# Copies of the bias rows with the 128 rows as outermost dimension, in a two-layer attention and feed-forward network

## The chip, the cores and the metric

The kernel runs on one core of one Trainium2 chip. The metric is the time of one execution on the device in microseconds (us), the median of the runs shown. A core has TensorE (PE; PEld is its weight load), VectorE (DVE), ScalarE (ACT), GpSimd (POOL) and SyncE (SP), and 16 DMA engines that move data. Most transfers here are issued by SP, one after the other, from one queue.

## What is computed

Two layers, each a mixer of attentions and a feed-forward net with a convolution, over 1024 tokens of width 1024, all in float32. What matters here is the first mixer and its biases: every attention adds a bias that depends on the distance of query and key alone.

```
def even_mixer(x, ...):                       # layer 0
    qa, ka, va, hb = split_cols(x @ w_in, ...)
    o_a = diff_attention(qa, ka, va, lam, bias_table[:, :4])
    o_b = dilated_mixture(hb, bias_table)     # 3 dilations (1, 4, 16) x 4 heads
    return concat(o_a, o_b) @ w_out

def banded_attention(q, k, v, max_dist, bias_tbl, dist_scale):
    dist = arange(blk)[:, None] + n_prev * blk - kj[None, :]
    bias = bias_tbl[t5_bucket(dist * dist_scale)]
    s = q @ k.T * D ** -0.5 + bias            # masked, softmax, times v
```

Layer 1 uses the same kind of bias with other heads (kinds "nat" and "win" below).

## The kernel before

A matrix product runs as three float32r products (high by high, high by low, low by high: `mm3`, lines 310, 312 and 314). A weight slab is loaded from DRAM by SP into one of two raw buffers (`wr`), ACT copies out its high part (`wh`, line 124) and DVE the low part (`wl`, line 125). ACT and DVE take their work in order, so a split that waits for its slab holds up all that stands behind it.

The even mixer goes through ten groups of heads: six dilated ones (three dilations, two pairs of heads each), then four of the difference attention. `dense` projects a group's v, q and k (48 matmuls of 512 columns each, tile `dn`) while `attend` does the scores (`sc`, line 757), the softmax and the products of the group before. The first group's projections run beside the making of the biases.

The biases go three steps. `bias_rows` (line 676) writes a table `R` in DRAM (in the trace `bias_rows`), one row per head, with the bias at every distance, kind after kind: it goes over the 5120 columns in ten pieces of 512, each with a load of a one-hot table (`th`, line 694, by POOL), a matmul (`sc`, line 696), a copy by ACT (`tl`, line 698) and a write by POOL (line 699). `skew` (line 702) copies a head's row 128 times into a DRAM tensor `sk_...`, so that `bias_tile` (line 712) can read it back with each partition shifted by one element. `skew` is called for "d0", "d1" and "d2" (the three dilations, four heads at a time, 384 columns), for "nat" (one head at a time, 1152 columns, eight heads) and for "win" (two heads at a time, 768 columns, four calls). The last four of "nat" and all of "win" are only read in layer 1.

All those copies are DRAM to DRAM and are issued by SP (`dma`, line 212), between the loads of weights. The order in which instructions stand on each engine is not the order of the code: the framework builds a schedule with a model of its own of what each instruction takes, and moves the copies to wherever the tables that they read are ready. `_row_kinds` (line 2014) gives the order of the kinds in `R`, and with it which of the ten pieces a copy waits for.

Of the kernel before, what the change touches and what calls it, by code (L numbers as in the profile page):

```python
# [192 lines left out]
class Net:  # L193
# [508 lines left out]
    def skew(self, kind, heads):  # L702

        off, w = ROWS[kind]
        t = self.dpool.tile([len(heads), 128, w], F32, name=f"sk_{kind}{heads[0]}")
        src = self.R[heads[0]:heads[0] + 1, off:off + w]
        self.dma(out=t, in_=bass.AP(tensor=src.tensor, offset=src.offset,
                                                  ap=[[ROWS_W, len(heads)], [0, 128], [1, w]]))
        for e, h in enumerate(heads):
            self.skews[kind, h] = t[e, :, :]  # L710

# [1301 lines left out]

def _row_kinds():
    kinds = {}
    n = np.arange(1152)
    kinds["nat"] = (1023 - n, (1023 - n) >= 0)
    n = np.arange(768)
    kinds["win"] = (639 - n, ((639 - n) >= 0) & ((639 - n) <= 511))
    n = np.arange(384)  # L2020
    dist = 255 - n
    ok = (dist >= 0) & (dist <= 128)
    kinds["d0"] = (dist, ok)
    kinds["d1"] = (dist * 4, ok)

    kinds["d2"] = (dist * 8, ok & (dist % 2 == 0))
    n = np.arange(2048)
    kinds["cmp"] = (n - 1039, (n - 1039) >= 0)
    return kinds


_KINDS = _row_kinds()
ROWS, ROWS_W = {}, 0
for _k, (_d, _v) in _KINDS.items():
# [80 lines left out]
```

## Time and profile before

| what | us |
|---|---|
| median of 3 runs | 2882.4 (2880.62 to 2885.14) |
| the profiled execution, whole | 2881.72 |
| its span | 2879.9 |
| PE busy in the span | 2691.6 (93%) |
| DVE / ACT / POOL busy | 1902.4 / 1341.0 / 528.4 |

The page is read as follows. The chain that ended last tells which engine the time hangs on, in shares of the span. Where that is one engine almost throughout, the stretches in which this engine is idle are looked for with the list of waits; the waits' releasers are followed to the engine, the line and in the end the transfer that came last; and the table by stretches tells what the DMA engines did meanwhile, as a mean busy share of all 16 (0.50 is half of them, or all half the time) and in GB/s, and at which clock PE was granted to run (1.00 is 2.4 GHz, 0.50 is 1.2 GHz).

### The profile page before, as it was taken

How to read it: one execution, taken by the hardware profiler on the slowest of the kernel's cores; microseconds unless marked ns; L12 is line 12 of the kernel's file. 1: busy time of each engine (PE TensorE's matmuls, PEld its weight loads, DVE VectorE, ACT ScalarE, POOL GpSimd, SP SyncE). 2: the span in 40 equal slices, each digit the busy share in tenths (PEclk: the TensorE clock that was granted, in tenths of full speed). 3: DMA queues.
4: the chain of work that ended last, by engine and by line, in shares of the span. 5: the costliest groups of instructions: out<-in, count | busy, mean ns of one | idle time of the engine just before them, and what ended most of it. 6: DMA issues, size and time to landing. Idle time of an engine off the chain costs nothing.

```text
span 2879.9 us, 37915 instructions
## 1 busy us (share of the span) xinstructions
PE 2691.6 (93%) x13415; PEld 2249.5 (78%) x13415; DVE 1902.4 (66%) x4139; ACT 1341.0 (47%) x2666; POOL 528.4 (18%) x673
## 2 busy tenths in 40 slices
PE   7299999979899999999999999899997999999998
PEld 5188888867788888888778788878786888888886
DVE  3155678878866666635563788778778766667346
ACT  3155566634444444312452588767644444444123
POOL 1011100022211111000101255444313111110002
PEclk8599999989899999999999999999998999999999
DMA  6211121412222224521432221021331222227121
GB/s 202 87 52 56 54 59 42 141 64 97 74 87 82 81 81 153 179 85 52 133 93 95 88 67 55 16 50 45 140 103 66 88 81 81 81 95 241 67 88 59
DMA packets 233612, 256.22 MB, mean 89 GB/s; under 512 B 49269, under 2 KB 189029, under 8 KB 233423
## 3 DMA queue, kind: packets, MB, share of 16 engines
q1 hardware_dynamic: 229199, 242.57, 26.0%
q0 software_dynamic: 4224, 11.23, 1.4%
q8 instruction: 106, 1.74, 0.3%
q14 instruction: 83, 0.68, 0.1%
HBM read 198.38 MB, written 65.60 MB: 92 GB/s over the span
## 4 chain that ended last, share of the span: by engine, by line
PE 80%; DVE 8%; SPq 3%; ACT 3%; issue 3%; DMA 2%; POOL 1%; DVEq 0%; POOLq 0%; ACTq 0%
PE u L310 9%; PE u L312 9%; PE u L314 9%; PE dn L310 6%; PE dn L312 6%; PE dn L314 6%; PE mm L312 6%; PE mm L310 6%; PE mm L314 6%; PE pt L980 4%; SPq L212 3%; PE sc L757 2%; PE po L1649 2%; PE sc L1593 1%; DVE g L288 1%
## 5 line engine op out<-in xcount | busy, mean ns | idle before, releaser
L446 ACT ACTIVATE wh<-wr 128x512 fp32r<-128x512 f32 x284 | 173.7, 628 | 564.6 <-PE u L312 298.0
L447 DVE TENSOR_TENSOR wl<-wr,wh 128x512 fp32r<-128x512 f32 x284 | 209.7, 752 | 99.4 <-ACT wh L446 98.5
L982 DVE TENSOR_TENSOR tl<-pt,th 128x512 fp32r<-128x512 f32 (+3 forms) x344 | 196.9, 587 | 32.7 <-ACT th L981 29.3
L981 ACT ACTIVATE th<-pt 128x512 fp32r<-128x512 f32 (+3 forms) x344 | 170.9, 517 | 98.2 <-PE pt L980 44.4
L370 DVE TENSOR_TENSOR x<-mm,x 128x1024 f32<-128x1024 f32 x64 | 78.3, 1223 | 173.9 <-PE mm L314 173.9
L627 POOL TENSOR_TENSOR x<-x 128x512 f32<-128x512 f32 x44 | 72.5, 1649 | 652.5 <-DVE x L626 652.5
L125 DVE TENSOR_TENSOR wl<-wr,wh 128x512 fp32r<-128x512 f32 (+3 forms) x118 | 94.5, 803 | 111.0 <-ACT wh L124 106.1
L298 POOL TENSOR_TENSOR x<-x,ln_b 128x1024 f32<-128x1024 f32 x25 | 60.1, 2403 | 546.3 <-ACT x L297 546.3
L446 ACT ACTIVATE wh<-s 128x512 fp32r<-128x512 f32 x132 | 83.5, 632 | 131.6 <-PE u L312 128.3
L124 ACT ACTIVATE wh<-wr 128x512 fp32r<-128x512 f32 (+3 forms) x118 | 77.2, 657 | 140.1 <-PE dn L312 65.6
L636 DVE SCALAR_TENSOR_TENSOR x<-x,cv,x 128x1023 f32<-128x1023 f32 x88 | 112.7, 1280 | 32.2 <-ACT x L633 32.2
L310 PE MATMUL dn<-xq0h,wh 128*128 128x512 f32 x176 | 73.6, 418 | 58.0 <-ACT kh L735 50.7
L761 DVE CUSTOM_DVE_ANT_0 s<-sc,bt 128x128 f32<-128x128 f32 (+3 forms) x192 | 81.6, 450 | 51.2 <-PE sc L757 29.7
L980 PE MATMUL pt<-ident,s 128*128 128x128 f32 x644 | 105.4, 278 | 0.9
L1013 POOL TENSOR_SCALAR s<-s,d_rd 128x128 f32<-128x128 f32 (+1 forms) x96 | 44.9, 485 | 280.6 <-DVE d_rd L1010 232.7
L447 DVE TENSOR_TENSOR wl<-s,wh 128x512 fp32r<-128x512 f32 x132 | 92.8, 703 | 0.1
L980 PEld LDWEIGHTS pt<-ident,s 128*128 128x128 f32 x644 | 76.3, 142 | 12.9 <-issue 5.5
L310 PEld LDWEIGHTS dn<-xq0h,wh 128*128 128x128 f32 x176 | 35.0, 199 | 65.0 <-ACT kh L735 51.0
L1593 PE MATMUL sc<-kh,q 128*128 128x256 f32 (+4 forms) x208 | 73.6, 359 | 11.0 <-DVE n_mx L761 8.3
L1649 PE MATMUL po<-tl,V 128*128 128x256 f32 x264 | 82.6, 333 | 0.0
L1649 PE MATMUL po<-th,V 128*128 128x256 f32 x264 | 76.2, 299 | 4.8 <-ACT th L981 4.8
L288 DVE SCALAR_TENSOR_TENSOR g<-x,ln_w,ln_g 128x1024 f32<-128x1024 f32 x32 | 76.9, 2404 | 5.7 <-ACT x L297 3.4
(541 smaller groups left out, 8817.1 us busy)
## 6 DMA issues: line engine op xcount, KB each, us to landing
wr<-in_ffn_w_up_dram SPq DMA_DIRECT2D x88, 512.0 KB
hid<-x SPq DMA_DIRECT2D x44, 512.0 KB
wr<-hid SPq DMA_DIRECT2D x44, 512.0 KB
wr<-in_ffn_w_down_dram SPq DMA_DIRECT2D x44, 512.0 KB
wr<-in_ev_w_in_dram SPq DMA_DIRECT2D x44, 256.0 KB
xres<-x SPq DMA_DIRECT2D x16, 512.0 KB
x<-xres SPq DMA_DIRECT2D x16, 512.0 KB
wr<-in_od_w_in_dram SPq DMA_DIRECT2D x15, 512.0 KB
```

The lines of the kernel that those rows point to most:

```text
L288: nc.vector.scalar_tensor_tensor(y, x, m, g, op0=OP.add, op1=OP.mult)
L310: nc.tensor.matmul(o, lhsT=sh, rhs=m[0], start=start, stop=False, **kw)
L312: nc.tensor.matmul(o, lhsT=sh, rhs=m[1], start=False, stop=False, **kw)
L314: nc.tensor.matmul(o, lhsT=sl, rhs=m[0], start=False, stop=stop, **kw)
L446: nc.scalar.activation(hi, v, AF.Copy)
L447: nc.vector.tensor_sub(lo, v, f32(hi))
L636: nc.vector.scalar_tensor_tensor(g[:, s:], c[:, :S - s], cv[:, 2 - s, f:f + 1], g[:, s:], op0=OP.mult, op1=OP.add)
L980: nc.tensor.transpose(pt[:k, e * 128:(e + 1) * 128], b, self.ident)
L981: nc.scalar.activation(th[:k, :n], pt[:k, :n], AF.Copy)
L982: nc.vector.tensor_sub(tl[:k, :n], pt[:k, :n], f32(th[:k, :n]))
L1593: nc.tensor.matmul(ps[:, :c1 - c0], lhsT=q, rhs=k[part][:, c0:c1], start=part == 0, stop=part == 1)
L1649: nc.tensor.matmul(po[:, :256], lhsT=v, rhs=parts[part][:, e * 256:(e + 1) * 256], start=first and e + part == 0, stop=last and e + part = ...
```

## The change

Two edits. In `skew`, source and destination are walked with the 128 copies as the outermost dimension and the heads inside it; before, the heads were outermost. The same bytes go to the same places, in as many pieces. In `_row_kinds`, the three dilated kinds get the first columns of `R` (0 to 1151), then "nat" (1152 to 2303), "win" (2304 to 3071) and "cmp" as before.

```
@@ skew
-        self.dma(out=t, in_=bass.AP(tensor=src.tensor, offset=src.offset,
-                                                  ap=[[ROWS_W, len(heads)], [0, 128], [1, w]]))
+
+        self.dma(out=t.rearrange("h r w -> r h w"), in_=bass.AP(tensor=src.tensor, offset=src.offset,
+                                                                ap=[[0, 128], [ROWS_W, len(heads)], [1, w]]))
@@ _row_kinds
     kinds = {}
-    n = np.arange(1152)
-    kinds["nat"] = (1023 - n, (1023 - n) >= 0)
-    n = np.arange(768)
-    kinds["win"] = (639 - n, ((639 - n) >= 0) & ((639 - n) <= 511))
     n = np.arange(384)
...
     kinds["d2"] = (dist * 8, ok & (dist % 2 == 0))
+    n = np.arange(1152)
+    kinds["nat"] = (1023 - n, (1023 - n) >= 0)
+    n = np.arange(768)
+    kinds["win"] = (639 - n, ((639 - n) >= 0) & ((639 - n) <= 511))
```

Since a copy waits for other pieces of `R` now, the schedule of the first stage comes out in another order. The first place is SP's queue in the first stage. Numbers behind a name tell buffers apart; `sk_d04` is the copy of dilation 0 from head 4, `wr_528` and `wr_534` are the second half of the v weights and the first half of the q weights of the second group. Before:

```order
L212 DMA sk_nat7_8020<-bias_rows_304 128x1x1152
L212 DMA sk_win0_8310<-bias_rows_304 256x1x768
L212 DMA sk_win2_8600<-bias_rows_304 256x1x768
L212 DMA sk_win4_8890<-bias_rows_304 256x1x768
L212 DMA sk_d04_470<-bias_rows_304 512x1x384
L212 DMA sk_win6_9180<-bias_rows_304 256x1x768
L212 DMA wr_528<-in_ev_w_in_dram 128x4x128
L212 DMA wr_534<-in_ev_w_in_dram 128x4x128
L212 DMA sk_d18_602<-bias_rows_304 512x1x384
L212 DMA sk_d212_1077<-bias_rows_304 512x1x384
L212 DMA bt_517<-sk_d04_470 128x256 x2
L212 DMA bt_941<-sk_d04_470 128x256 x2
```

After, from the end of the first group's weights on:

```order
L212 DMA sk_d04_470<-bias_rows_304 128x4x384
L212 DMA sk_d18_602<-bias_rows_304 128x4x384
L212 DMA sk_d212_1077<-bias_rows_304 128x4x384
L212 DMA wr_455<-in_ev_w_in_dram 128x4x128
L212 DMA bt_517<-sk_d04_470 128x256 x2
L212 DMA bt_941<-sk_d04_470 128x256 x2
L212 DMA sk_nat0_1558<-bias_rows_304 128x1152
L212 DMA sk_nat1_2017<-bias_rows_304 128x1152
L212 DMA sk_nat2_2446<-bias_rows_304 128x1152
L212 DMA sk_nat3_2912<-bias_rows_304 128x1152
L212 DMA sk_nat4_7150<-bias_rows_304 128x1152
L212 DMA wr_528<-in_ev_w_in_dram 128x4x128
```

and behind that:

```order
L212 DMA sk_nat5_7440<-bias_rows_304 128x1152
L212 DMA sk_nat6_7730<-bias_rows_304 128x1152
L212 DMA sk_nat7_8020<-bias_rows_304 128x1152
L212 DMA sk_win0_8310<-bias_rows_304 128x2x768
L212 DMA wr_534<-in_ev_w_in_dram 128x4x128
L212 DMA sk_win2_8600<-bias_rows_304 128x2x768
L212 DMA sk_win4_8890<-bias_rows_304 128x2x768
L212 DMA sk_win6_9180<-bias_rows_304 128x2x768
L212 DMA wr_619<-in_ev_w_in_dram 128x4x128
L212 DMA wr_625<-in_ev_w_in_dram 128x4x128
```

The dilated copies and the bias tiles of the first two groups of heads 4 to 7 (`bt`) have moved from behind all others to the front; `wr_528` stands behind five copies of "nat", `wr_534` behind the eighth and one of "win", and `wr_619` and `wr_625` behind all.

The second place is PE in the first stage, where `sc_376` is the matmul of the seventh piece of `R` (its one-hot table is `th_374`) and `pt_...` are the transposes of the last input tiles. Before:

```order
L696 MATMUL sc_369<-th_367,tblp_306 16x512
L240 MATMUL pt_232<-ident_67,s_230 128x128 x4
L696 MATMUL sc_376<-th_374,tblp_306 16x512
L240 MATMUL pt_239<-ident_67,s_230 128x128 x4
L240 MATMUL pt_248<-ident_67,s_246 128x128 x4
L696 MATMUL sc_390<-th_388,tblp_306 16x512
L240 MATMUL pt_255<-ident_67,s_246 128x128 x4
L310 MATMUL dn_381<-xq2h_126,wh_275 128x512
```

After, further on in the q projection of the first group:

```order
L314 MATMUL dn_457<-xq1h_124,wl_292 128x512
L310 MATMUL dn_457<-xq1h_124,wh_291 128x512
L312 MATMUL dn_457<-xq1l_125,wh_291 128x512
L314 MATMUL dn_457<-xq1h_124,wl_292 128x512
L696 MATMUL sc_376<-th_374,tblp_306 16x512
L310 MATMUL dn_457<-xq1h_124,wh_291 128x512
L312 MATMUL dn_457<-xq1l_125,wh_291 128x512
L312 MATMUL dn_381<-xq2l_127,wh_275 128x512
L314 MATMUL dn_381<-xq2h_126,wl_276 128x512
```

All sixteen of those transposes and nineteen matmuls of the projections stand ahead of `sc_376` now; before, four of the transposes did.

## Rows read from the trace of the kernel before

**Rows 1.** The page's fourth part: the chain that ended last, by engine.
```profile
PE 80%; DVE 8%; SPq 3%; ACT 3%; issue 3%; DMA 2%; POOL 1%; DVEq 0%; POOLq 0%; ACTq 0%
```

**Rows 2.** Waits of PE, 20 to 150 us (total us, times, longest).
```profile
PE dn L310 <- ACT kh L735: 50.7, 1, 50.7
PE sc L696 <- DMA th<-in_c_onehot_dram: 9.3, 1, 9.3
PE sc L757 <- DVE dm L761: 7.7, 2, 7.4
```

**Rows 3.** PE, in time (start, us, instruction, idle before and releaser).
```profile
35.97 0.59 PE L696 MATMUL sc<-th,tblp 97*16 97x512 f32 x1 [9.32 <-DMA th<-in_c_onehot_dram]
...
120.35 0.80 PE L310 MATMUL dn<-xq0h,wh 128*128 128x512 f32 x1 [50.75 <-ACT kh L735]
...
121.37 0.63 PE L314 MATMUL dn<-xq0h,wl 128*128 128x512 f32 x1
121.79 0.63 PE L310 MATMUL dn<-xq0h,wh 128*128 128x512 f32 x1
...
126.81 0.39 PE L310 MATMUL dn<-xq1h,wh 128*128 128x512 f32 x1
127.03 0.39 PE L312 MATMUL dn<-xq1l,wh 128*128 128x512 f32 x1
```

**Rows 4.** ACT, in time, 60 to 124 us.
```profile
118.28 1.40 ACT L124 ACTIVATE wh<-wr 128x512 fp32r<-128x512 f32 x2 [52.47 <-DMA wr<-in_ev_w_in_dram]
```

**Rows 5.** SP's queue, in time, 18 to 140 us: start and time of issue.
```profile
23.33 1.87 SPq L212 DMA_DIRECT2D sk_nat<-bias_rows  x3
...
27.86 3.73 SPq L212 DMA_DIRECT2D sk_nat<-bias_rows  x5
37.70 31.11 SPq L212 DMA_DIRECT2D sk_win<-bias_rows  x3
68.91 14.84 SPq L212 DMA_DIRECT2D sk_d<-bias_rows  x1
83.80 11.40 SPq L212 DMA_DIRECT2D sk_win<-bias_rows  x1
95.30 14.86 SPq L212 DMA_DIRECT2D wr<-in_ev_w_in_dram  x2
...
119.04 10.04 SPq L212 DMA_DIRECT2D bt<-sk_d  x4
```

**Rows 6.** Stretches: length, busy us (instructions) by engine; then PEclk, DMA share, GB/s.
```profile
28.00:30.00 2.00, 0.00 (x0) 0.00 (x0) 0.70 (x2) 0.58 (x2) 0.42 (x1) 0.90 0.80 221
...
34.00:36.00 2.00, 0.03 (x1) 0.06 (x2) 0.00 (x0) 0.00 (x0) 0.00 (x0) 0.50 1.11 339
...
38.00:40.00 2.00, 1.87 (x8) 1.16 (x6) 1.38 (x2) 0.67 (x3) 0.00 (x0) 0.54 0.72 177
...
72.00:76.00 4.00, 0.00 (x0) 0.00 (x0) 0.00 (x0) 0.00 (x0) 0.00 (x0) 0.75 0.13 52
...
88.00:92.00 4.00, 0.00 (x0) 0.00 (x0) 0.00 (x0) 0.00 (x0) 0.00 (x0) 0.50 0.26 103
```

**Rows 7.** The same view, later stretches.
```profile
136.20:142.46 6.26, 5.92 (x18) 4.81 (x19) 5.50 (x23) 4.48 (x13) 1.76 (x4) 0.52 0.17 49
...
250.00:350.00 100.00, 100.00 (x544) 85.95 (x543) 59.46 (x154) 58.26 (x149) 16.04 (x36) 1.00 0.20 57
```

**Rows 8.** POOL, in time, 14 to 56 us: loads of the one-hot table.
```profile
25.34 1.77 POOL L694 DMA_DIRECT2D th<-in_c_onehot_dram  x3 [5.73 <-PE sc L696]
```

**Rows 9.** The chain that ended last, in time (start, us, what).
```profile
27.10 10.59 DMA bias_rows<-tl
```

**Rows 10.** DMA issues by line, with their count and size.
```profile
sk_nat<-bias_rows SPq DMA_DIRECT2D x8, 576.0 KB
sk_win<-bias_rows SPq DMA_DIRECT2D x4, 768.0 KB
wr<-in_ev_w_in_dram SPq DMA_DIRECT2D x44, 256.0 KB
```

## The prediction

> **What bounds the kernel now.** I read the chain that ended last first: PE holds 80% of it, SP's queue 3% [rows 1]. So time is won where PE stands idle, and the list of PE's waits says where in the first 150 us: 50.7 us for ACT's `kh`, 9.3 us for a one-hot table, 7.7 us for DVE's maxima `dm` [rows 2]. Later nothing of the kind comes: from 250 to 350 us PE is busy for 100.00 of 100 us [rows 7]. What PE gains early it should therefore keep.
>
> Then I follow the largest wait back. PE stops at 69.6 us and goes on at 120.35 [rows 3]. ACT has not written `kh` because a weight split stands ahead of it in its order, and that split waited 52.47 us for its slab `wr` [rows 4]. The slab was late on SP's queue: eight copies of "nat" (one head each) were issued in about 0.6 us apiece, but three of "win" (two heads each) held the queue for 31.11 us, one of `sk_d` 14.84, the last of "win" 11.40, and only then, at 95.30, came the two slabs [rows 5]. The table by stretches says why. While "nat" was moving, the DMA share was 0.80 to 1.11 and 221 to 339 GB/s; with only "win" under way it was 0.13, or 2 of 16 engines, and 52 GB/s; when the dilated copy had joined, 0.26, 4 of 16, and 103 GB/s [rows 6]. A copy is spread by its outermost dimension: two heads use two engines, four use four, 128 rows use all. The queue is held because these few engines are backed up. The 7.4 us behind the first wait are of one cause with it: the bias tiles were issued at 119.04 behind the dilated copies [rows 5], and DVE could not make its maxima without them.
>
> **The change part by part.** The new outer dimension is 128 for every copy, so I take "win" and the dilated copies to move as "nat" did. Terms, against the profiled execution (2881.7 us whole; the median of the runs is 2882.4, 0.7 above):
>
> 1. The 50.75 us wait goes if the slabs land before PE asks (checked below).
> 2. The 7.7 us wait for `dm` goes: the dilated copies and their bias tiles are now first in the queue, needing only the first three pieces of `R`, which were what "nat" needed before, issued at 23.33 [rows 5], so the bias tiles are there before 40 us, and PE wants them near 60.
> 3. After each long idle PE ran at half clock: 512-column matmuls start 0.42 to 0.43 us apart after 121 us, and 0.22 to 0.23 us apart at full clock [rows 3]. Eleven starts of the first stretch lose 0.2 us each, 2.3 us; the stretch from 136.20 to 142.46 (granted clock 0.52, 18 matmuls) [rows 7] loses about 2.4. Together 4.7 us, which go with the idles.
> 4. The 9.3 us wait was for the seventh one-hot table, issued with two others at 25.34 [rows 8]; its matmul started at 35.97 [rows 3], because "nat" filled the engines. Now sixteen transposes and nineteen matmuls stand ahead of that matmul where four transposes did. The nineteen take 4.4 us at 0.23, the other transposes some 3 (an estimate), so PE comes to it near 34 instead of 26.7. If the table lands no later than before, at most 2 us of waiting are left; with it go 1.5 us of half clock behind the idle. Between nothing and all 10.8 us, I take 10.8 less 2.
>
> Sum of all four: 50.75 + 7.7 + 4.7 + 10.8 = 74 us.
>
> What is late next? The full-width copies fill the engines, and slabs queue behind them. "nat" now needs the fourth and fifth pieces of `R`; the fourth took 10.59 us to land and was there at 37.70 [rows 9]. So SP stands still before the first copy of "nat" until 34 to 38 us; I take 37. The dilated copies and tiles, issued from about 22, have drained by then. Behind come eight "nat" at 576 KB, four "win" at 768 KB and three slabs at 256 KB before `wr_619` is through [rows 10]: 4608 + 3072 + 768 = 8448 KB, 8.65 MB. At the mean of the four stretches from 28 to 36 us, 276 GB/s [rows 6], that is 31 us: `wr_619` lands at about 70 and `wr_625`, which needs a free raw buffer, a microsecond or two later. By the same count `wr_528` lands near 50 and `wr_534` near 60.
>
> When are they wanted? PE used to end the first group's projections at 69.6; less term 4 that is 59 to 63. `wr_528` and `wr_534` are wanted from then on and are there. ACT and DVE split `wr_619` and `wr_625` ahead of evacuations that PE needs after eight scores of half the width (1 us), 24 matmuls of v at 0.23 (5.5), twelve scores (1.4), and 24 more matmuls with seven transposes (6.5), so at about 74 to 77. The slack is 3 to 7 us. I charge 4 us for all of it, the 2 us at the table included: gain 74 - 4 = 70 us, profile 2811.7, median about 2812.
>
> The bound downwards is all 74 us and a few more from order alone: 2804. Upwards, the slowest stretch with copies queued is 177 GB/s [rows 6]: 8.65 MB take 49 us, `wr_619` lands near 88, PE waits 11 to 14 us: 74 - 4 - 14 = 56, so 2826; with half of the one-hot wait kept, 2831.
>
> **The rivals.**
>
> A. *The copies starve the loads* (that upper end): 2820 to 2831. For it: with "nat" under way the share was 1.11 [rows 6] and a small write took 10.59 us [rows 9], and now 7.9 MB move in one piece just as the second group's weights are due. Against it: the rate held at 276, and the slack. The Trainium skill (DMA: Bandwidth & Descriptors, Where 436 GB/s comes from) gives HBM about 358 GB/s per core; a copy from DRAM to DRAM reads and writes there, so by an estimate from that page it would run at 179 GB/s, and the result would be rival A's 2826. The stretch at 34 us shows 339 GB/s [rows 6], so the measurement is against it.
>
> B. *The outer dimension doesn't spread these copies.* No row shows a copy of several heads with 128 outside. Then three dilated copies run on four engines, 768 KB at 103 GB/s [rows 6], 7.6 us each, and hold the queue from 22 to 45; "nat" drains by about 63; four "win" at 52 GB/s take 15 us each, and `wr_619` lands near 126. PE waits some 52 us: 74 - 4 - 52 = 18, so 2864. Still faster, because the dilated tiles come first and the stall is one, not two. The Trainium skill (DMA: Bandwidth & Descriptors, Why a DMA increments its semaphore by 16 and not by 1) says that the number of engines is the largest up to 16 that divides both sides' slowest dimension that isn't 1; by that this rival has no chance. The shares 0.13 and 0.26 agree with 2 and 4.
>
> C. *Slower.* All sixteen engines read the same few source rows at once, and if the source were the limit, "win" and the dilated copies would run at the 52 GB/s of two engines however many take part, and hold up all 16 engines instead of two. 8.65 MB at 52 GB/s are 166 us; `wr_619` lands near 205, PE waits about 131: 2881.7 - 74 + 4 + 131 = 2943. It decides below about 82 GB/s, where the stall eats the 70 us (8.65 MB in the 105 us from 37 to about 142). Against it: "nat" reads one row with all engines at 221 to 339 GB/s.
>
> **How the numbers follow.** The forecast, 2804 to 2820, gets 0.71; A 0.22; B 0.04; C 0.03. The forecast's own time is the prediction, 2812. The range takes in the forecast and A, 2804 to 2831, and leaves out B and C. A measurement of this kernel can tell about 0.2%, 6 us, from no change. The forecast, A and B are all faster by more; C is slower; between them, by some price in B and C that I have not thought of, 0.01 is left for no change. Faster 0.96, same 0.01, slower 0.03.
>
> **What would show it.** On SP's queue every copy takes about 0.6 to 0.7 us to issue, none above 2, and the first two dilated copies go out before 25 us. The DMA share is near 1 from about 37 to 68 us and no stretch stays at 0.13. PE has no wait for `kh` or `dm` above 5 us, is at full clock from 40 us on, and starts the second group's v projection near 61 to 65 us instead of 120.35. From there to the end the two traces differ by a constant. I am wrong if ACT's split still waits over 10 us for a slab (A), if a copy is issued in over 5 us (B), or if PE's gain at 150 us is not there at the end.

## The result, and the profile after

The changed kernel takes 2817.3 us (median of 4 runs, 2815.3 to 2819.2) beside 2881.8 us for the kernel before on the same chip. The ratio is 0.9777 with a 95% interval of 0.9765 to 0.9789: faster by 64.5 us. The forecast was 2812, its own range 2804 to 2820, and the range with rival A 2804 to 2831. The profiled execution took 2819.23 us with a span of 2817.5, so the working below is made against that: 2881.7 - 2819.2 = 62.5 us.

First PE's waits between 20 and 150 us, as in [rows 2] (total us, times, longest):

```profile
PE dn L310 <- DVE q L727: 3.6, 1, 3.6
PE dn L310 <- ACT kh L736: 1.5, 1, 1.5
```

The waits for `kh` (50.7), the one-hot table (9.3) and `dm` (7.7) are gone. These two are new, and the prediction didn't have them; the waits below them are 1.4 us and less. SP's queue, as in [rows 5] (start, time of issue), from the dilated copies on:

```profile
23.74 1.98 SPq L212 DMA_DIRECT2D sk_d<-bias_rows  x3
...
39.26 3.64 SPq L212 DMA_DIRECT2D sk_nat<-bias_rows  x5
42.99 0.55 SPq L212 DMA_DIRECT2D wr<-in_ev_w_in_dram  x1
43.59 2.03 SPq L212 DMA_DIRECT2D sk_nat<-bias_rows  x3
46.61 0.56 SPq L212 DMA_DIRECT2D sk_win<-bias_rows  x1
49.40 0.39 SPq L212 DMA_DIRECT2D wr<-in_ev_w_in_dram  x1
51.64 10.74 SPq L212 DMA_DIRECT2D sk_win<-bias_rows  x3
62.48 33.59 SPq L212 DMA_DIRECT2D wr<-in_ev_w_in_dram  x7
```

Three dilated copies go out in 1.98 us where one took 14.84; three of "win" in 10.74 where three took 31.11. The slabs `wr_528` and `wr_534`, which were issued from 95.30 on before, go out at 42.99 and 49.40, and `wr_619` is the first of the seven at 62.48. The stretches, as in [rows 6] (length, busy us and instructions of PE, PEld, DVE, ACT and POOL; PEclk, DMA share, GB/s):

```profile
36.00:40.00 4.00, 4.00 (x18) 3.13 (x18) 0.00 (x0) 0.91 (x2) 0.59 (x2) 1.00 1.07 359
...
56.00:60.00 4.00, 0.97 (x3) 0.85 (x4) 3.12 (x5) 2.23 (x5) 0.00 (x0) 0.93 0.92 190
...
64.00:68.00 4.00, 3.27 (x19) 2.67 (x17) 0.00 (x0) 0.48 (x1) 0.00 (x0) 1.00 1.07 355
...
136.20:142.46 6.26, 6.26 (x38) 5.53 (x37) 4.45 (x14) 2.33 (x4) 0.00 (x0) 1.00 0.03 10
```

No stretch stays at 0.13 or 0.26. Over the nine stretches of 4 us from 36 to 72 the mean share is 0.95 (lowest 0.71) and the mean rate 279 GB/s. From 136.20 to 142.46, where PE ran 18 matmuls at half clock [rows 7], it now runs 38 at full clock.

Where the gain arises is read off the first instruction at a fixed point of the program. The writes of `O`, the results of the six dilated groups, are such points (duration of the issues, then start of the first and of the last). Before and after:

```profile
L212 SPq DMA_DIRECT2D op_dram<-O x6: 338/338/339, 186.1 to 397.9; - x6
```

```profile
L212 SPq DMA_DIRECT2D op_dram<-O x6: 338/338/339, 121.5 to 333.2; - x6
```

That is 64.6 us earlier, and the last one 64.7. The whole kernel ends 62.5 us earlier. So all of the gain is made in the first 120 us. The 2 us that this trace gives back later are not in the second trace of the changed kernel (after_again below): there the first write comes 65.1 us earlier and the span ends 64.8 us earlier, so they lie within what two executions of one kernel differ by.

Finally the two new waits. PE in time (start, us, instruction, idle before and releaser):

```profile
55.04 0.39 PE L314 MATMUL dn<-xq1h,wl 128*128 128x512 f32 x1
59.03 0.47 PE L310 MATMUL dn<-xq2h,wh 128*128 128x512 f32 x1 [3.60 <-DVE q L727]
...
60.51 0.63 PE L312 MATMUL dn<-xq2l,wh 128*128 128x512 f32 x1
60.94 0.63 PE L314 MATMUL dn<-xq2h,wl 128*128 128x512 f32 x1
...
68.82 0.50 PE L310 MATMUL dn<-xq0h,wh 128*128 128x512 f32 x1 [1.54 <-ACT kh L736]
```

and ACT in the same stretch:

```profile
55.46 0.63 ACT L124 ACTIVATE wh<-wr 128x512 fp32r<-128x512 f32 x1 [7.57 <-PE dn L314]
56.11 0.59 ACT L726 ACTIVATE q<-dn 64x512 fp32r<-64x512 f32 x1
...
67.52 0.63 ACT L124 ACTIVATE wh<-wr 128x512 fp32r<-128x512 f32 x1 [6.68 <-DMA wr<-in_ev_w_in_dram]
68.17 0.59 ACT L736 ACTIVATE kh<-dn 64x512 fp32r<-64x512 f32 x1
...
75.63 0.63 ACT L124 ACTIVATE wh<-wr 128x512 fp32r<-128x512 f32 x1 [1.10 <-DMA wr<-in_ev_w_in_dram]
```

ACT stands at a weight split from 47.9 to 55.46, and the evacuation of q stands behind it. An evacuation copies a finished product out of PSUM, where PE writes; PE needs it for its next matmul into the same buffer. The releaser named there is a matmul of PE, but the slab is the likelier one: `wr_528` was issued at 42.99 and took 12.4 us to land, which is 55.4. A run below shows the same split let go by the slab. The second split waited for `wr_534`, issued at 49.40 and 18.1 us under way; the k evacuation stands behind it. It is the pattern of [rows 4], much smaller: 7.57 and 6.68 us where it was 52.47, and PE loses only 3.6 and 1.5 of them. Behind the first wait PE's matmuls start 0.43 us apart until 62.65, which costs about 1.7 us more.

### The profile page after: what moved, and what is told of

Same layout as the page of the kernel before. It is cut to its first block, busy times and chain, and to the rows that moved or that the text cites. A ratio compares the mean times of both kernels' runs of the same rounds, so it can differ in the third digit from the quotient of the medians.

```text
span 2817.5 us, 37908 instructions
## 1 busy us (share of the span) xinstructions
PE 2686.5 (95%) x13415; PEld 2245.4 (80%) x13415; DVE 1899.9 (67%) x4139; ACT 1340.4 (48%) x2666; POOL 529.1 (19%) x673
## 4 chain that ended last, share of the span: by engine, by line
PE 49%; DVE 6%; ACT 3%; issue 2%; DMA 1%; SPq 0%; POOL 0%; DVEq 0%; ACTq 0%; POOLq 0%
PE mm L312 6%; PE mm L314 6%; PE mm L310 6%; PE u L314 5%; PE u L310 5%; PE u L312 5%; PE pt L981 3%; PE dn L310 3%; PE dn L312 3%; PE dn L314 3%; PE po L1650 2%; PE sc L1594 1%; DVE g L288 1%; PE po L1909 1%; DVE tl L983 1%
## 5 line engine op out<-in xcount | busy, mean ns | idle before, releaser
L125 DVE TENSOR_TENSOR wl<-wr,wh 128x512 fp32r<-128x512 f32 (+3 forms) x118 | 94.3, 801 | 75.3 <-ACT wh L124 64.7
L981 PEld LDWEIGHTS pt<-ident,s 128*128 128x128 f32 x644 | 76.1, 142 | 12.4 <-issue 5.3
L310 PE MATMUL dn<-xq2h,wh 128*128 128x512 f32 x176 | 71.1, 404 | 3.6 <-DVE q L727 3.6
```

The source lines that it names most:

```text
L310: nc.tensor.matmul(o, lhsT=sh, rhs=m[0], start=start, stop=False, **kw)
L981: nc.tensor.transpose(pt[:k, e * 128:(e + 1) * 128], b, self.ident)
```

## The experiments

The theory was that the shape of the copies does nearly all of it: with two or four engines under way, SP's queue stands still, and slabs and bias tiles behind it come late. The first rival was that the order of the rows does it, because it puts the dilated copies and the bias tiles ahead of the copies for layer 1. All times stand against runs of the kernel before on the same chip: 2880.2 us for the first four, 2880.0 for the next pair, 2882.2 for the last.

### outer_alone: the shape, without the new order of rows

```
@@ skew (the kernel before)
-        self.dma(out=t, in_=bass.AP(... ap=[[ROWS_W, len(heads)], [0, 128], [1, w]]))
+        self.dma(out=t.rearrange("h r w -> r h w"), in_=bass.AP(... ap=[[0, 128], [ROWS_W, len(heads)], [1, w]]))
```

> The 128 copies outermost, the rows of R in the order of before: the instructions stand in the order of before on every engine, only the shape of the copies differs. If the stall came from copies on two and four engines (theory), no copy takes over 5 us to issue, the slabs wr_528 and wr_534 land near 61 us, PE's wait of 50.7 us for kh is gone, the wait for dm is under 4 us, and the 9.3 us at the one-hot table stay: 50.75 + 7.7 + 4.7 - 0 to 4 = 60 us faster than before, about 2822 (2816 to 2830). If the order of the rows did it (rival), under half of the 64 us is seen: over 2850.

Measured: 2819.3 us (2816.7 to 2819.7), ratio 0.9788 [0.9774, 0.9801]. PE's waits from 20 to 150 us, and rows of SP's queue:

```profile
PE sc L696 <- DMA th<-in_c_onehot_dram: 7.6, 1, 7.6
PE sc L758 <- DVE dm L762: 0.8, 1, 0.8
PE dn L310 <- ACT kh L736: 0.3, 1, 0.3
```

```profile
38.39 2.68 SPq L212 DMA_DIRECT2D sk_win<-bias_rows  x3
...
43.23 4.41 SPq L212 DMA_DIRECT2D sk_win<-bias_rows  x1
47.74 7.69 SPq L212 DMA_DIRECT2D wr<-in_ev_w_in_dram  x2
...
62.74 4.45 SPq L212 DMA_DIRECT2D bt<-sk_d  x4
```

With every instruction in the order of the kernel before, 60.9 us go. The waits for `kh` and `dm` fall from 58.4 to 1.1 us together; the wait for the one-hot table stays, at 7.6. So the shape alone takes the large stall, and the table is the rows' part.

### order_alone: the new order of rows, the heads outermost as before

```
@@ skew (the changed kernel)
-        self.dma(out=t.rearrange("h r w -> r h w"), in_=bass.AP(... ap=[[0, 128], [ROWS_W, len(heads)], [1, w]]))
+        self.dma(out=t, in_=bass.AP(... ap=[[ROWS_W, len(heads)], [0, 128], [1, w]]))
```

> The dilated rows first, the heads still outermost in the copies: the instructions stand in the order of after on every engine. Theory (the number of engines is the cause): the copies of win hold SP's queue again for 13 to 15 us each, wr_619 lands near 126 us, PE waits some 50 us there, the wait for dm and most of the one-hot wait are gone: about 2864 (2855 to 2874), rival B's sum. If the order did it: 2817.

Measured: 2876.8 us (2874.0 to 2878.8, 10 runs), ratio 0.9988 [0.9979, 0.9997]: 3.4 us faster than before, 13 us above the expectation and outside its range. PE's waits, SP's queue, and one stretch:

```profile
PE dn L310 <- ACT vt L742: 31.2, 1, 31.2
PE pt L747 <- ACT vt L742: 11.7, 1, 11.7
PE dn L310 <- ACT kh L736: 10.9, 1, 10.9
PE dn L310 <- DVE q L727: 4.6, 1, 4.6
```

```profile
22.65 13.81 SPq L212 DMA_DIRECT2D sk_d<-bias_rows  x3
36.55 8.07 SPq L212 DMA_DIRECT2D wr<-in_ev_w_in_dram  x1
...
61.22 16.83 SPq L212 DMA_DIRECT2D wr<-in_ev_w_in_dram  x1
78.11 30.52 SPq L212 DMA_DIRECT2D sk_win<-bias_rows  x3
```

```profile
84.00:88.00 4.00, 0.00 (x0) 0.00 (x0) 0.00 (x0) 0.00 (x0) 0.00 (x0) 0.62 0.13 52
```

The stall of 0.13 and 52 GB/s is back, and SP stands on the same "win" copies for 30.52 us. The one-hot wait is gone, but PE waits 58.4 us for other evacuations, of the same cause: ACT's splits wait 81.3 us for slabs here, in six waits, against 52.5 in one before. The expectation was rival B's sum, which had one stall at `wr_619`; in the run `wr_455` and `wr_534`, behind the dilated copies and the first of "win", are held for 8.07 and 16.83 us as well. The order of rows without the shape is worth little, since it only decides which slab stands behind the slow copies.

### eight_engines: every copy as one head with eight outermost

```
@@ skew (the changed kernel)
-        self.dma(out=t.rearrange("h r w -> r h w"), in_=bass.AP(... ap=[[0, 128], [ROWS_W, len(heads)], [1, w]]))
+        for e in range(len(heads)):
+            self.dma(out=t[e].rearrange("(a r) w -> a r w", a=8), in_=bass.AP(
+                ... offset=src.offset + e * ROWS_W, ap=[[0, 8], [0, 16], [1, w]]))
```

> After, with every head copied by a transfer of its own whose outermost dimension is 8 (16 copies inside it). If the outermost dimension sets the number of engines (theory): with only copies under way the DMA share is near 0.5 and the rate near 206 GB/s (8 times the 26 GB/s an engine of the two-engine stretch), against a share near 1 and 260 GB/s in after; the slabs land some 9 us later: about 2826 (2820 to 2836; the schedule puts the one-hot matmul early again, which can cost up to 9 of it). If the engines are shared out in another way: share near 1 and 2817.

Measured: 2830.6 us (2828.1 to 2832.1), ratio 0.9828 [0.9814, 0.9841]. Two stretches while the copies move, and PE's waits:

```profile
44.00:48.00 4.00, 4.00 (x19) 3.17 (x18) 0.69 (x1) 1.11 (x2) 0.11 (x1) 1.00 0.53 212
...
64.00:68.00 4.00, 3.93 (x18) 2.92 (x16) 0.00 (x0) 0.00 (x0) 0.00 (x0) 1.00 0.50 208
```

```profile
PE sc L758 <- ACT kh L736: 6.1, 1, 6.1
PE sc L696 <- DMA th<-in_c_onehot_dram: 4.0, 2, 3.2
PE dn L310 <- ACT kh L736: 3.3, 1, 3.3
```

In six of the seven stretches of 4 us from 40 to 68 us the share is 0.50 to 0.55 and the rate 201 to 221 GB/s (in the seventh 0.63 and 239): an outermost dimension of eight gives eight engines. Together with [rows 6] that is 2, 4 and 8 engines at 52, 103 and some 208 GB/s. What the outermost dimension decides is thereby shown at three sizes, and at 128 by the shares near 1 above. The Trainium skill (DMA: Bandwidth & Descriptors, Why a DMA increments its semaphore by 16 and not by 1) says that the engines are the largest number up to 16 that divides the slowest dimension of both sides that isn't 1; the four sizes agree (shares 0.13, 0.26, 0.50 to 0.55, and 0.95 in the mean). The kernel is 13.7 us slower than the changed one (2816.8, measured apart): copies at three quarters of the rate hold the slabs longer, and PE waits 9.4 us for `kh` behind late slabs. Not all of it is the rate: some 40 rows of PE stand elsewhere in the first stage, and 4.0 us of waiting for one-hot tables are back.

### late_copies: the copies for layer 1 held back until the feed-forward net

The two new waits were put down to slabs behind copies. Eight of the copies (the last four of "nat" and all of "win") aren't read before layer 1. Here each first gets 16 bytes of a tile `cv` of layer 0's feed-forward net, so it can't be issued before that stage; all but some 30 rows of PE stand in the order of the changed kernel.

```
@@ skew (the changed kernel), and its calls in the feed-forward net
+        if late is not None:
+            self.dma(out=t[0, 0:1, 0:4], in_=late)
...
-                    spare[f // 2]()
+                    spare[f // 2](cv[0:1, 0, 0:4])
```

> After, with the eight copies that only layer 1 reads (heads 4 to 7 of nat, all of win) held back to the feed-forward stage of layer 0, by a 16-byte write into each from a tile that is made there. Theory (what is left of PE's waits in after, 3.6 and 1.5 us at 55 to 69 us and 2 us of half clock, comes from slabs queued behind these copies): the waits go, wr_528 lands before 52 us, 7 us faster than after, about 2810 (2807 to 2813), the moved copies hidden under the feed-forward products. If the slabs are late of themselves (raw buffers, their short pieces): 2817, the same as after.

Measured: 2814.9 us (2812.2 to 2816.1), ratio 0.9772 [0.9758, 0.9785]. PE's waits in the first stage, the split on ACT, and a stretch where the copies now run:

```profile
PE sc L696 <- DMA th<-in_c_onehot_dram: 1.2, 1, 1.2
PE dn L310 <- DVE q L728: 0.7, 1, 0.7
```

```profile
51.63 1.38 ACT L124 ACTIVATE wh<-wr 128x512 fp32r<-128x512 f32 x2 [5.38 <-DMA wr<-in_ev_w_in_dram]
```

```profile
620.00:630.00 10.00, 6.94 (x33) 5.21 (x32) 8.53 (x14) 5.59 (x10) 5.35 (x4) 0.92 0.80 268
```

The new waits fall from 5.1 to 0.7 us, and the first write of `O` comes at 115.0 us, 6.5 ahead of the changed kernel (in late_again below, the same kernel once more, at 117.2, 4.3 ahead). So the copies in front of the slabs were their cause. The same split now ends its wait with the slab, at 51.63, while PE is busy: that is why the slab, and not the matmul named, is taken as its releaser after the change too. But the time, 2814.9 us, is above the 2807 to 2813 that were expected, and the end is only 4.1 us ahead in the profiles. 2.5 us were lost on the way, and by the same reading of fixed points this happens between 596 and 700 us, where the moved copies run at a share of 0.80. That the copies cost it there was only argued so far; two more kernels, and this one once more, were run for it.

### mid_copies, and the changed kernel again: the eight copies inside the mixer

```
@@ even_mixer (the changed kernel, with late in skew as above)
+            mids = [("nat", [h]) for h in range(4, 8)] + [("win", [h, h + 1]) for h in range(0, 8, 2)]
...
+                if 2 <= n:
+                    self.skew(*mids[n - 2], late=f32(G[key]["k"][0][0])[0:1, 0:4])
```

and the calls in the feed-forward net fall away.

> The whole change as it is, but the eight copies that only layer 1 reads (nat of heads 4 to 7 and the four of win) are issued one per group of heads in the even mixer, each held back by a 16-byte write from that group's kh into the copy's own tensor. In that stretch PE was busy for 100 of 100 us and the DMA share was about 0.2. Theory: what late_copies gained in the first 120 us (first write of O 6.5 us ahead of the changed kernel) is lost again only because the moved copies ran beside the layer norm and the feed-forward weights; beside the mixer they cost nothing, so all 6.5 us are kept: 2811 us (2808 to 2813), the first writes of O and of the odd layer's tiles all 6 to 7 us ahead. Rival: a copy of this size costs PE some 0.3 us wherever it runs, by the weight loads that it delays: 2815 us (2813 to 2817), like late_copies, with the loss spread over the mixer between 120 and 450 us.

> The changed kernel itself beside mid_copies on the same chip, so that 3 to 6 us can be told apart: 2817 us (2815 to 2819.5), with no wait of PE above 6 us in the first 150 us.

Measured: mid_copies 2818.2 us (2815.3 to 2821.3), the changed kernel beside it 2816.8 (2815.4 to 2818.8), ratios 0.9784 [0.9770, 0.9797] and 0.9779 [0.9765, 0.9792]. Theory and rival both missed: it isn't faster than the changed kernel at all. Fixed points, mid_copies and then the changed kernel (`xres` is written behind the mixer, eight times in each layer):

```profile
L212 SPq DMA_DIRECT2D op_dram<-O x6: 338/339/345, 116.6 to 328.3; - x6
...
L212 SPq DMA_DIRECT2D xres<-x x16: 319/320/339, 599.7 to 2133.9; - x16
```

```profile
L212 SPq DMA_DIRECT2D op_dram<-O x6: 338/338/339, 121.0 to 332.8; - x6
...
L212 SPq DMA_DIRECT2D xres<-x x16: 319/320/339, 602.0 to 2129.9; - x16
```

At 116.6 it is 4.4 us ahead, at 328.3 still 4.5, so beside the mixer the copies cost nothing. At 599.7 it is 2.3 ahead, at 2133.9 it is 4.0 behind. The last moved copy is issued at 482.9, and at 499.2, where `v` is loaded from `op_dram`, the kernel is still 4.3 ahead: the loss lies in places where no moved copy runs. But in this kernel the schedule had changed too: several hundred rows of PE stand elsewhere, around 600, 1400 and 2100 us. Two things were changed at once, so the run couldn't tell.

### mixer_copies and late_again: the same with nothing else moved

The calls of `skew` stay where they are in the code, and each copy gets its 16 bytes from the part of `op_dram` that a dilated group has written. Now all of PE, DVE, ACT and POOL behind the first stage stand in the order of the changed kernel.

```
@@ the calls in the feed-forward net (the changed kernel, with late in skew as above)
+        mark = lambda i: net.opd[i, 0:1, 0:4]
-        spare = [lambda: None] + [lambda h=h: net.skew("nat", [h]) for h in range(4, 8)]
-        spare += [lambda h=h: net.skew("win", [h, h + 1]) for h in range(0, 8, 2)]
+        spare = [lambda: None] + [lambda h=h, i=i: net.skew("nat", [h], mark(i)) for h, i in zip(range(4, 8), (0, 1, 2, 4))]
+        spare += [lambda h=h, i=i: net.skew("win", [h, h + 1], mark(i)) for h, i in zip(range(0, 8, 2), (3, 5, 5, 5))]
```

> As mid_copies, the eight copies for layer 1 go out inside the even mixer, but now each waits for a write of O of a dilated group (16 bytes of that write are copied into the copy's own tensor first), and all other instructions of PE, DVE, ACT and POOL behind the first 150 us stand in the order of the changed kernel; in mid_copies some 500 rows of PE stood elsewhere, in the stretches in which it lost. Theory: in mid_copies it was that order, and not the copies, that gave 9 us back behind the mixer; so here the 5 to 6.5 us that are gained before 120 us stay to the end: 2811.5 us (2809 to 2813.5). Rival: copies beside the mixer delay what layer 1 needs, whatever the order: 2815 to 2818 us, and the loss is seen between 500 and 700 us and behind 1390 us, as in mid_copies.

> The kernel of late_copies again, beside mixer_copies on the same chip: 2815 us (2812.5 to 2817). Theory: 3 to 4 us slower than mixer_copies, because the copies run beside the layer norm at 609 to 623 us. Rival: the same time as mixer_copies.

Measured: mixer_copies 2812.7 us (2812.1 to 2814.8), ratio 0.9764 [0.9751, 0.9777]; late_again 2814.3 us (2812.3 to 2817.5), ratio 0.9768 [0.9755, 0.9781]. The fixed points of mixer_copies, and then of late_again:

```profile
L212 SPq DMA_DIRECT2D op_dram<-O x6: 338/338/339, 115.6 to 327.4; - x6
...
L212 SPq DMA_DIRECT2D xres<-x x16: 319/320/339, 597.6 to 2126.1; - x16
```

```profile
L212 SPq DMA_DIRECT2D op_dram<-O x6: 338/339/339, 117.2 to 328.9; - x6
...
L212 SPq DMA_DIRECT2D xres<-x x16: 319/323/349, 598.6 to 2127.0; - x16
```

mixer_copies is 5.4 us ahead of the changed kernel at both points of the mixer, 4.4 at the first `xres` and 3.8 at the last. Most of the 9 us that mid_copies gave back (from 4.4 ahead to 4.4 behind) are gone with its order. Apart from the order, the two kernels differ in which 16 bytes hold a copy back, and so in when it goes out; so the order is the likely cause, but it rests on one trace of each, taken on different chips, and the trace of mid_copies is the slowest of its four runs (2821.3, median 2818.2). Which of the moved instructions does it was not looked for.

mixer_copies has the lowest median here, about 4 us under the changed kernel (by the ratios, 0.0013 to 0.0015 of 2880 us), and it is ahead at every fixed point read, but the intervals of the two ratios overlap. Between mixer_copies and late_again the 1.5 us can't be told from nothing. And the loss that mid_copies and mixer_copies were made to explain is hardly there in late_again: it is 3.8 us ahead of the changed kernel beside mid_copies at the first write of `O`, 3.4 at the first `xres` and 2.9 at the end. So whether the copies cost anything beside the layer norm stays open.

## Why the prediction was right, and where it was off

**What bounds, and why the queue stood still.** Right. The shares 0.13 and 0.26 were read as 2 and 4 engines; order_alone brings both the share and the 30.52 us issue back, and outer_alone takes them away, with the order of everything unchanged. What makes an issue of SP wait stands in no row; that the times of the issues follow the shape is shown.

**Term 1, the 50.75 us wait.** Right: gone, and what is left for `kh` is 1.5 us. **Term 2, the 7.7 us for `dm`.** Right: no such row. In outer_alone it falls to 0.8 with the bias tiles still behind the other copies, so the copies' speed was enough, and their new place, on which the prediction leant, was not needed. **Term 3, 4.7 us at half clock.** Right for both stretches: PEclk is 1.00 from 136.20 to 142.46. But 1.7 us of the kind came back behind the new wait at 59.03, where full clock was expected from 40 us on.

**Term 4, the one-hot wait and its half clock, 10.8 us.** Right as a term: the wait is gone, and in outer_alone, with the old order, it is still 7.6 us. But what it gained was spent at once. outer_alone starts the second group's v projection at 68.51 and the changed kernel at 68.82:

```profile
68.51 0.50 PE L310 MATMUL dn<-xq0h,wh 128*128 128x512 f32 x1 [0.28 <-ACT kh L736]
```

In the changed kernel PE comes to the first new wait 6.4 us earlier (it starts the last matmul ahead of it at 55.04, outer_alone the same one at 61.46), and then waits for the slabs. In this stretch the drain of the copies sets the pace, and the order of rows is worth at most the 2 to 3 us between 2819.3 and 2817, which these runs can't tell from nothing.

**What is late next.** This step failed in its size, in two ways. First, the prediction said that `wr_528` and `wr_534` are wanted from 59 to 63 us "and are there". It looked for when PE needs the slabs. But ACT splits them ahead of evacuations that PE needs sooner: it stood at the first from 47.9 and at the second from 60.8 us. Second, they land later than estimated: 55.4 and 67.5 instead of 50 and 60, and `wr_619` at 75.6 instead of 70. The queue's first copy of "nat" went out at 39.26 instead of 37, and then it took 36 us instead of 31 until `wr_619` was there. In these 36 us the engines moved 9.47 MB at 260 GB/s: the rate was a little under the 276 that were taken, and 0.8 MB, tables and the end of the dilated copies among them, were not in the count of 8.65 MB. The third dilated copy, which should have drained by 37, landed at 40.2. So the second group's v projection started at 68.82, not between 61 and 65. `wr_619`, whose slack was worked out, cost PE no wait; but the v projection ahead of it began 4 to 8 us later than forecast, so that is luck, and doesn't show that the slack was there. The charge of 4 us for all that was late should have been 10: 3.6 + 1.5 us of waits, 1.7 of half clock, and some 3 around 27 to 32 us (two waits of 1.4 and 0.6 for the transposes' copies, and starts at half clock). 74 - 10 = 64, which is what the first write of `O` shows (64.6). The time stayed within the forecast's own range because 6 us are little beside 74.

**The gain is kept.** Right as far as two traces tell: 64.6 us at 121.5 and 62.5 at the end in one, 65.1 and 64.8 in the other. The prediction had the traces differ by a constant.

**The rivals.** A, that the copies starve the loads, came true in small: ACT's splits wait 7.57 and 6.68 us, each under the 10 that was set as its mark, and 14.25 together. late_copies shows that it is the copies. The estimate of 179 GB/s from the Trainium skill (DMA: Bandwidth & Descriptors, Where 436 GB/s comes from) isn't borne out: "nat" and "win" alone, 7.9 MB from 39.26 to 75.6 us, make 217 GB/s. B is excluded by the issues; only the last two of "win" exceed the 2 us that were expected at most (10.74 us for three). C is excluded by the rate.

## What to carry to other kernels

Where a queue of transfers stands still, compare the DMA share with the fraction of engines that the outermost dimension can occupy: 0.13 of the engines at full work looks idle on average and blocks everything issued behind. When such a stall is taken away, ask not only when the bound engine needs the next late transfer, but when the in-order engine in front of it comes to it, and what stands behind it there. And an edit that moves one transfer can reorder the rest of a scheduled program: compare two versions only when the other instructions stand in the same order.

## What the runs showed of the hardware

The rate of these copies is proportional to the engines up to eight, and grows by less beyond. Two, four and eight engines move 52, 103 and 208 GB/s, 26 each. Sixteen moved a mean of 279 GB/s at a share of 0.95, which is 17 each (single stretches of 4 us show 190 to 359); some other loads and writes are in that. So at sixteen a busy engine moves less than at eight; what binds there wasn't tested.

Full width does not free the queue altogether. Behind many copies SP's issues still stretch (the last three of "win" took 10.74 us together), and a slab of 256 KB, 2.9 us from issue to landing in the median of the changed kernel, takes 12.4 and 18.1 us there. Holding back copies that nobody needs yet took most of the waits away that this made: 5.1 us became 0.7 and 1.0.
